# One decoder layer on one core: both heads' attention scores in one two-bank PSUM tile, small products issued as unbroken runs

## The chip, the cores and the metric

The kernel runs on one core of one Trainium2 chip. The metric is the device time of one execution in microseconds (us): lower is better. The time before is a median of three runs. A change of less than 0.2% (about 0.9 us) can't be told from none with this kernel.

## The reference, cut to what matters

The layer takes x (256 positions, 1024 channels, float32). After an RMS norm, one wide projection gives the queries, keys and values of three attention mixers with 64 channels a head, and merge gates; the mixers' outputs are projected, gated, merged, projected once more and added to x. Then come a gated feed-forward layer with a short convolution and a final norm.

```
def decoder(x):
    h = rmsnorm(x);  all = h @ w_in                      # q, k, v of A, B, C, and gates
    o_a = banded attention, 3 groups of 2 heads          # one softmax over all bands per head
    o_b = gate0 * compressed + gate1 * selected + gate2 * window    # 6 query heads, 2 kv heads
    o_c = causal attention, 4 heads
    x = x + (sum of sigmoid(gate) * (o @ w_branch)) @ w_out
    x = x + (silu(conv(u)) * conv(v)) @ w_down           # u, v = rmsnorm(x) @ w_up
    return rmsnorm(x)

# scores of one head: a query tile of 128 positions against the keys that it may see
s = q @ k.T * 0.125 + bias[distance];  p = softmax(s);  o = p @ v

# compression of B: 15 overlapping blocks of 32 positions, flattened to 2048, for k and for v
hidden = gelu(flat @ w1)      # (15 * 2 heads, 2048) @ (2048, 256)
cmp = hidden @ w2
```

## The kernel before, in words

**Projections.** Activations lie with channels on the partitions, split into a high and a low part (`hn_hi`, `hn_lo`). Weights come in units of up to 1 MB (`raw`), are split by ScalarE (`whi`, line 223) and VectorE (`wlo`, line 227), and each product of a projection is three matmuls into a PSUM tile `g` (`mm3`, lines 239 to 241), mostly 128 by 128 against 256 columns. There are four buffers of `raw`, two of each split, two PSUM banks of `g`. These projections fill TensorE for most of the kernel.

**Attention.** `scores` (line 437) computes one pair of heads. A pair lies in one 128-partition tile, head 0 on partitions 0 to 63 and head 1 on 64 to 127, and so its products contract over 64 rows. Two blocks are needed for causal attention: the first 128 queries against 128 keys (128 columns), the last 128 queries against 256 keys (256 columns). Each float32 product is two TensorE instructions, so that a pair of heads makes eight. The scores of each head go to a PSUM tile `s` of its own, of one bank; the pool `ps_s` has two. VectorE reads them with `add_max` (line 447: adds the bias, takes the maximum, writes to SBUF), ScalarE takes the exponentials (491 or 518), VectorE scales (498 or 522), TensorE transposes (454) into PSUM tile `t`, ScalarE copies to `pT` (456), and `pv` (462) multiplies with the values into PSUM tile `o`, which `put_o` (478, 479) evicts. The softmax of B and C works in SBUF tiles `tt`, of which there are three.

`scores` is called 11 times: three times for mixer A (loop at line 506), six for B (line 626: three pairs, selected and window branch each), two for C (line 643). One more user of `s` is B's compressed branch: two tiles, one for each half of the queries (line 596). The first projection also borrows one (line 382).

**Compression.** `hidden(i)` (line 532) loads one eighth of `w1` (512 KB, tile `gl`, four buffers, line 535) and multiplies it in four products that use 32 columns of the array each, into one PSUM tile `ph`. The first four eighths come ahead of unit b0, the other four between b0 and b1; the first of all has `start`, the last `stop`.

**Order.** The program is traced in this order, and a planner then fixes each engine's order ahead of time: it keeps a simulated clock, and an engine takes, of the instructions whose inputs are ready by that clock, the one with the lowest priority number, which is the order of tracing. Each engine then runs its list strictly in that order and waits at semaphores. In `manual_schedule` the instructions of a block keep the order in which they were traced on the engines named, but others may come between them. Projections of later units are therefore put between attention's products as filler. Memory and PSUM of the mixers are given back after the gates of the first half are traced (line 659), and the branch projections (line 722) come after that.

Of the kernel before, what the change touches and what calls it, by code (L numbers as in the profile page):

```python
# [10 lines left out]
F32 = mybir.dt.float32  # L11
# [5 lines left out]
P = 128  # L17
WARM = 16
S = 256
# [72 lines left out]
def _unit_places():  # L92

    at, places = 0, {}
    for name, _, rows, cols in _unit_list():
        k, n = sum(r for _, r in rows) // P, sum(c for _, c in cols)
        places[name] = (at, k, n)
        at += P * k * n
    return places, at
# [28 lines left out]
def decoder_layer(ctx: ExitStack, tc, x, small_b, table, w1, wts, norms, out):  # L128
    nc = tc.nc
    out = out[0]  # L130
    places, _ = _unit_places()
# [6 lines left out]
    psg = ctx.enter_context(tc.tile_pool(name="psg", bufs=2, space=bass.MemoryType.PSUM))  # L138
# [96 lines left out]
    def unit(name, steps=2, eng=None):  # L235
        return Unit(name).split(steps, eng)
# [6 lines left out]
    mix = ctx.enter_context(tc.tile_pool(name="mix", bufs=1))  # L243
    o_hi = mix.tile([P, KC, S], F32R, name="o_hi")
    o_lo = mix.tile([P, KC, S], F32R, name="o_lo")
    mixer = ctx.enter_context(ExitStack())
    qkv = mixer.enter_context(tc.tile_pool(name="qkv", bufs=1))
    att = mixer.enter_context(tc.tile_pool(name="att", bufs=1))
    ps_s = mixer.enter_context(tc.tile_pool(name="ps_s", bufs=2, space=bass.MemoryType.PSUM))
    ps_t = mixer.enter_context(tc.tile_pool(name="ps_t", bufs=2, space=bass.MemoryType.PSUM))  # L250
    ps_o = mixer.enter_context(tc.tile_pool(name="ps_o", bufs=2, space=bass.MemoryType.PSUM))


    idle = att.tile([P, 384], F32, name="tt", bufs=3)[:, :P]
# [83 lines left out]
    def chunk_T(view, pool=psg):  # L338

        ps = pool.tile([P, 512], F32, name="g")[:, :S]  # L340
        for i, k in enumerate(K_ORDER):
            mm3(ps, view(0, k), view(1, k), h_hi[:, k, :], h_lo[:, k, :], i == 0, i == KC - 1)
        return ps

    def chunks_hi_first(views, pss):

        half_k = range(KC // 2), range(KC // 2, KC)
        for a, b, ks in ((0, h_hi, range(KC)), (1, h_hi, half_k[0]), (0, h_lo, half_k[0]),
                         (1, h_hi, half_k[1]), (0, h_lo, half_k[1])):
            for k in ks:  # L350
                for view, ps in zip(views, pss):
                    nc.tensor.matmul(ps, view(a, k), b[:, k, :], start=(a == 0 and b is h_hi and k == 0),
                                     stop=(b is h_lo and k == KC - 1))

    def to_sbuf(ps, name, scale=1.0):
        o = qkv.tile([P, S], F32, name=name)
        nc.scalar.activation(o, ps, AF.Copy, scale=scale)
        return o

    def plain(u, c):  # L360
        return lambda part, k: u[part][:, k, c * P:(c + 1) * P]
# [17 lines left out]
    for i in range(3):  # L379
        if i == 0:  # L380
            u = u_a0.views
            pss = [p.tile([P, 512], F32, name=n)[:, :S] for p, n in ((psg, "g"), (ps_s, "s"))]
            chunks_hi_first([plain(u, c) for c in range(2)], pss)
        else:
            u = u_a1.views if i == 1 else unit(f"a{i}")
            pss = [chunk_T(plain(u, c)) for c in range(2)]
        for c in range(2):
            j = 2 * i + c
            aT.append(to_sbuf(pss[c], f"aT{j}", 0.125 if j < 3 else 1.0))
# [32 lines left out]
    flat = att.tile([P, 2, 16, 32], F32, name="flat")  # L422
    nc.vector.memset(flat, 0.0)
    for w in range(2):
        ps = chunk_T(plain(u, w))
        for kv in range(2):
            for odd in range(2):
                rows = slice(64 * odd, 64 * odd + 64)
# [5 lines left out]
    V1 = proj_V("v1", 512, "V1")  # L434


    def scores(q, k):

        pss = [ps_s.tile([P, 512], F32, name="s")[:, :384] for _ in range(2)]
        for q0, k1, o in ((0, P, slice(0, 128)), (P, S, slice(128, 384))):  # L440
            for i in range(2):
                rows = slice(64 * i, 64 * i + 64)
                nc.tensor.matmul(pss[i][:, o], q[rows, q0:q0 + P], k[rows, 0:k1], start=True, stop=True)  # L443
        return pss

    def add_max(dst, ps, bias, m):
# [12 lines left out]
    def o_tile():  # L459
        return ps_o.tile([P, 512], F32, name="o")[:, :S]  # L460

    def pv(po, terms, more=()):

        steps = []
        for pT, v, v0 in terms:
            steps.append([(slice(0, S), v[:, 0, v0[h]:v0[h] + 64], pT[h][:, 0:256]) for h in range(2)])
            steps.append([(slice(P, S), v[:, 1, v0[h]:v0[h] + 64], pT[h][:, 256:384]) for h in range(2)])
        steps += [[(slice(0, S), *m[h]) for h in range(2)] for m in more]  # L470
        with tc.manual_schedule(engines={mybir.EngineType.PE}):
            for i, step in enumerate(steps):
                for h in (1, 0):
                    cols, a, b = step[h]
                    nc.tensor.matmul(po[64 * h:64 * h + 64, cols], a, b, start=i == 0, stop=i == len(steps) - 1)  # L475

    def put_o(po, c):
        nc.scalar.activation(o_hi[:, c, :], po, AF.Copy)
# [46 lines left out]
    for g in range(3):  # L525
        po = o_tile()
# [2 lines left out]

    ph = o_tile()  # L530

    def hidden(i):

        wt = mix.tile([P, 4, S], F32, name="gl", bufs=4)
        nc.sync.dma_start(wt, w1[i])
        for grp in range(4):
            nc.tensor.matmul(ph[32 * grp:32 * grp + 32, :], flat[:, grp // 2, 2 * i + grp % 2, :], wt[:, grp, :],  # L537
                             start=(i == 0), stop=(i == 7))

    for i in range(4):  # L540
        hidden(i)


    u = unit("b0")
    bq = [to_sbuf(chunk_T(plain(u, c)), f"bq{c}", 0.125) for c in range(2)]
    for i in range(4, 8):
        hidden(i)
    u = unit("b1")
    bq.append(to_sbuf(chunk_T(plain(u, 0)), "bq2", 0.125))
    bks = to_sbuf(chunk_T(plain(u, 1)), "bks")  # L550
# [41 lines left out]


    pcT = att.tile([96, 2, S], F32, name="pcT")
    for t in range(NT):
        ps = ps_s.tile([P, 512], F32, name="s")[:, :96]
        for c in range(3):
            nc.tensor.matmul(ps[:, 32 * c:32 * c + 32], bq[c][:, t * P:(t + 1) * P], kcmp, start=True, stop=True)
        ps = ps.rearrange("p (c kv b) -> p kv c b", c=3, kv=2)
        wide = att.tile([P, 6, 32], F32, name="sc", bufs=2)  # L600
        nc.vector.memset(wide, 0.0)
        sc = wide[:, :, 0:16]
        mk = sb_[:, B_MK + 32 * t:B_MK + 16 + 32 * t][:, None, :].to_broadcast([P, 3, 16])
        ok = sb_[:, B_MK + 16 + 32 * t:B_MK + 32 + 32 * t][:, None, :].to_broadcast([P, 6, 16])
        for kv in range(2):
            nc.vector.tensor_add(sc[:, 3 * kv:3 * kv + 3, :], ps[:, kv], mk)
        m = small.tile([P, 6], F32, name="m6")
        nc.vector.tensor_reduce(m, sc[:, :, 0:15], axis=AX.X, op=ALU.max)
        nc.vector.tensor_sub(sc, sc, m[:, :, None].to_broadcast([P, 6, 16]))
        nc.scalar.activation(sc, sc, AF.Exp)  # L610
        z = small.tile([P, 6], F32, name="z6")
        nc.vector.tensor_reduce(z, sc[:, :, 0:15], axis=AX.X, op=ALU.add)
        nc.vector.tensor_mul(z, z, gsel[:, t, :, 0])
        nc.vector.reciprocal(z, z)
        nc.vector.tensor_mul(sc, sc, ok)
        nc.vector.tensor_mul(sc, sc, z[:, :, None].to_broadcast([P, 6, 16]))
        pp = ps_t.tile([P, 512], F32, name="t")[:96, :S].rearrange("p (a q) -> p a q", a=2)
        for a in range(2):
            nc.tensor.transpose(pp[:, a, :], wide[:, 3 * a:3 * a + 3, :].rearrange("p h b -> p (h b)"), ident)
        nc.vector.tensor_copy(pcT[:, :, t * P:(t + 1) * P], pp)  # L620

    for c in range(3):
        po = o_tile()
        pT = {}
        for w, k in ((1, bks), (2, bkw)):
            for kv, ps in enumerate(scores(bq[c], k)):
                h = c + 3 * kv
# [13 lines left out]
    for j in range(2):  # L641
        po = o_tile()
# [5 lines left out]
    def gates(i, pool):  # L648

        gl = [pool.tile([P, 4, S], F32, name="gl", bufs=4)[:, 0:3, :] for _ in range(2)]  # L650
        for b in range(3):
            u = unit(f"g{i}{b}")
            for c in range(2):
                nc.scalar.activation(gl[c][:, b, :], chunk_T(plain(u, c)), AF.Copy)  # L654
        return gl

    gl = {i: gates(i, mix) for i in range(2)}
# [7 lines left out]
    def gtile():  # L665
        turn[0] ^= 1
        return pools[turn[0]].tile([P, 512], F32, name="g")[:, :S]
# [34 lines left out]
    for i in range(4):  # L702
# [10 lines left out]
        for c in range(2):  # L713
# [5 lines left out]
            for b, (k0, k1) in enumerate(branch_k):  # L719
                ps = gtile()  # L720
# [25 lines left out]
    rows, scaled = spare[1][:, 0:S], [spare[1][:, i * S:(i + 1) * S] for i in range(1, 4)]  # L746
# [43 lines left out]
    with tc.manual_schedule(engines={mybir.EngineType.Activation, mybir.EngineType.DVE, mybir.EngineType.Pool,  # L790
# [49 lines left out]
        for i in range(4):  # L840
            for k in range(KC):
                u = fu[("fa0", "fu0")[i % 2]]
                nc.tensor.matmul(firsts[i], u[1][:, k, i // 2 * P:(i // 2 + 1) * P], h_hi[:, k, :], start=False,  # L843
                                 stop=k == KC - 1)
# [21 lines left out]
    for i in range(NFF // 2):  # L866
        with tc.issue_after(on_act[3 + i].ins) if i in (1, 2) else ExitStack():
            ua, uu, ud = [fu.pop(f"f{w}{i}", None) or unit(f"f{w}{i}") for w in "aud"]
        for c in range(2):
            ch = 2 * i + c  # L870

            def up(u):
                ps = gtile()
                for k in range(KC):
                    mm3(ps, u[0][:, k, c * P:(c + 1) * P], u[1][:, k, c * P:(c + 1) * P],
                        h_hi[:, k, :], h_lo[:, k, :], k == 0, k == KC - 1)
                return by_rstd(ps)
            a = conv(firsts[2 * ch] if ch < 2 else up(ua), ch)
            sa = mpool.tile([P, S], F32, name="sa")
            nc.scalar.activation(sa, a, AF.Silu)  # L880
            b = conv(firsts[1] if ch == 0 else by_rstd(firsts[3]) if ch == 1 else up(uu), NFF + ch)
# [45 lines left out]
```

## Time and profile before

| what | us |
|---|---|
| median of 3 runs | 437.43 (437.16 to 437.55) |
| profiled execution, its own time | 438.12 |
| span of its instructions | 436.3 |
| TensorE busy (matmuls) | 426.7 |
| VectorE busy | 306.9 |
| ScalarE busy | 240.8 |

The profiled execution is 0.69 us above the median of the runs, and its time is 1.8 us above its span. In the rows below, PE is TensorE, PEld its loading of weights, DVE VectorE, ACT ScalarE and SPq the queue that issues DMAs. `x8` counts instructions. Matmuls are pipelined: a row's duration runs until its last result, so one starts while those before it still run, and what a product takes from TensorE is read from one start to the next.

### The profile page before, as it was taken

How to read it: one execution, taken by the hardware profiler on the slowest of the kernel's cores; microseconds unless marked ns; L12 is line 12 of the kernel's file. 1: busy time of each engine (PE TensorE's matmuls, PEld its weight loads, DVE VectorE, ACT ScalarE, POOL GpSimd, SP SyncE). 2: the span in 40 equal slices, each digit the busy share in tenths (PEclk: the TensorE clock that was granted, in tenths of full speed). 3: DMA queues.
4: the chain of work that ended last, by engine and by line, in shares of the span. 5: the costliest groups of instructions: out<-in, count | busy, mean ns of one | idle time of the engine just before them, and what ended most of it. 6: DMA issues, size and time to landing. Idle time of an engine off the chain costs nothing.

```text
span 436.3 us, 7726 instructions
## 1 busy us (share of the span) xinstructions
PE 426.7 (98%) x3104; PEld 390.5 (89%) x3104; DVE 306.9 (70%) x637; ACT 240.8 (55%) x421; POOL 12.9 (3%) x19
## 2 busy tenths in 40 slices
PE   8999999999999999999999999999999999999993
PEld 7998877987789998999998998999999999999982
DVE  5756752888575588647535899897797797887854
ACT  6443362558676782456344769465465464573423
POOL 3301000000000000000000000000000000000001
PEclk9999999999999999999999999999999999999997
DMA  8988647340226785525550185753652743700002
GB/s 290 388 333 317 227 160 264 116 174 15 84 97 243 290 335 206 220 108 194 194 192 2 50 337 183 299 202 131 246 201 95 285 173 118 290 0 2 2 0 96
DMA packets 12611, 78.09 MB, mean 179 GB/s; under 512 B 1392, under 2 KB 1408, under 8 KB 4640
## 3 DMA queue, kind: packets, MB, share of 16 engines
q1 hardware_dynamic: 12000, 75.48, 46.6%
q0 software_dynamic: 576, 2.12, 1.4%
q8 instruction: 24, 0.39, 0.4%
q14 instruction: 11, 0.09, 0.1%
HBM read 76.52 MB, written 1.07 MB: 178 GB/s over the span
## 4 chain that ended last, share of the span: by engine, by line
PE 93%; DMA 2%; issue 1%; POOL 1%; DVE 1%; ACT 1%; POOLq 0%; SPq 0%
PE g L241 21%; PE g L239 21%; PE g L240 21%; PE acc L239 6%; PE acc L240 6%; PE acc L241 6%; PE s L443 3%; PE o L475 2%; PE t L454 2%; PE g L787 2%; DMA raw<-in_wts_dram 2%; PE o L537 1%; PE g L843 1%; POOL wlo L227 1%; PE acc L760 0%
## 5 line engine op out<-in xcount | busy, mean ns | idle before, releaser
L227 DVE TENSOR_TENSOR wlo<-raw,whi 128x1024 fp32r<-128x1024 f32 (+2 forms) x130 | 152.9, 1205 | 50.4 <-ACT whi L223 49.9
L239 PE MATMUL g<-hn_hi,wlo 128*128 128x256 f32 x632 | 180.6, 286 | 0.0
L241 PE MATMUL g<-hn_hi,whi 128*128 128x256 f32 x632 | 179.9, 285 | 0.0
L240 PE MATMUL g<-hn_lo,whi 128*128 128x256 f32 x632 | 179.9, 285 | 0.0
L223 ACT ACTIVATE whi<-raw 128x1024 fp32r<-128x1024 f32 (+2 forms) x130 | 129.3, 1038 | 38.2 <-PE g L241 28.1
L239 PEld LDWEIGHTS g<-hn_hi,wlo 128*128 128x128 f32 x632 | 121.1, 192 | 3.8 <-issue 2.3
L240 PEld LDWEIGHTS g<-hn_lo,whi 128*128 128x128 f32 x632 | 121.0, 192 | 2.7 <-issue 1.9
L241 PEld LDWEIGHTS g<-hn_hi,whi 128*128 128x128 f32 x632 | 121.1, 192 | 1.4 <-issue 1.3
L862 DVE SCALAR_TENSOR_TENSOR cy<-xn,small_b,cy 128x255 f32<-128x255 f32 (+1 forms) x88 | 41.7, 480 | 10.8 <-ACT cy L860 9.8
L860 ACT ACTIVATE cy<-xn,small_b 128x256 f32<-128x256 f32 x44 | 26.1, 594 | 17.2 <-DVE xn L776 17.2
L239 PE MATMUL acc<-whi,fl 128*128 128x512 f32 x88 | 34.5, 393 | 0.0
L240 PE MATMUL acc<-wlo,fh 128*128 128x512 f32 x88 | 34.4, 391 | 0.0
L241 PE MATMUL acc<-whi,fh 128*128 128x512 f32 x88 | 34.2, 389 | 0.0
L885 ACT ACTIVATE fh<-sa 128x256 fp32r<-128x256 f32 x22 | 9.1, 413 | 33.1 <-DVE sa L882 33.1
L776 DVE TENSOR_TENSOR xn<-g,xn 128x256 f32<-128x256 f32 x44 | 18.5, 420 | 9.6 <-PE g L241 9.0
L654 ACT ACTIVATE gl<-g 128x256 f32<-128x256 f32 x24 | 9.1, 381 | 24.1 <-PE g L241 24.1
L241 PEld LDWEIGHTS acc<-whi,fh 128*128 128x128 f32 x88 | 16.5, 188 | 3.6
L239 PEld LDWEIGHTS acc<-whi,fl 128*128 128x128 f32 x88 | 16.6, 188 | 3.1
L240 PEld LDWEIGHTS acc<-wlo,fh 128*128 128x128 f32 x88 | 16.6, 189 | 2.8
L240 PE MATMUL g<-o_lo,whi 128*128 128x256 f32 x64 | 18.1, 283 | 0.0
L241 PE MATMUL g<-o_hi,whi 128*128 128x256 f32 x64 | 18.1, 283 | 0.0
L239 PE MATMUL g<-o_hi,wlo 128*128 128x256 f32 x64 | 18.1, 283 | 0.0
(180 smaller groups left out, 505.4 us busy)
## 6 DMA issues: line engine op xcount, KB each, us to landing
raw<-in_wts_dram SPq DMA_DIRECT2D x62, 1024.0 KB, 4.9
gl<-in_w_dram SPq DMA_DIRECT2D x8, 512.0 KB, 7.5
raw<-in_wts_dram SPq DMA_DIRECT2D x2, 804.0 KB, 8.3
raw<-in_wts_dram SPq DMA_DIRECT2D x3, 512.0 KB, 7.2
T<-tvd POOLq DMA_DIRECT2D x1, 1280.0 KB, 13.3
xs<-in_x_dram SPq DMA_DIRECT2D x2, 516.0 KB, 3.8
out_dram<-raw SPq DMA_DIRECT2D x4, 256.0 KB, 2.2
T<-tvd POOLq DMA_DIRECT2D x1, 768.0 KB, 8.2
```

The source lines that it names most:

```text
L223: nc.scalar.activation(self.parts[0][:, sl], self.raw[:, sl], AF.Copy)
L227: return (eng or nc.vector).tensor_sub(self.parts[1][:, sl], self.raw[:, sl], self.parts[0][:, sl].bitcast(F32))
L239: nc.tensor.matmul(ps, al, bh, start=start, stop=False)
L240: nc.tensor.matmul(ps, ah, bl, start=False, stop=False)
L241: nc.tensor.matmul(ps, ah, bh, start=False, stop=stop)
L443: nc.tensor.matmul(pss[i][:, o], q[rows, q0:q0 + P], k[rows, 0:k1], start=True, stop=True)
L454: nc.tensor.transpose(ps[:, i * P:(i + 1) * P], b, ident)
L654: nc.scalar.activation(gl[c][:, b, :], chunk_T(plain(u, c)), AF.Copy)
L776: nc.vector.tensor_mul(u, ps, rows)
L860: on_act.append(nc.scalar.activation(y, u, AF.Identity, bias=vec_c[:, 3, ch:ch + 1], scale=vec_c[:, 2, ch:ch + 1]))
L862: nc.vector.scalar_tensor_tensor(y[:, sh:], u[:, :S - sh], vec_c[:, w, ch:ch + 1], y[:, sh:], op0=ALU.mult, op1=ALU.add)
L885: nc.scalar.activation(fh, sa, AF.Copy)
```

## The change

Both heads of a pair now share one tile `s` of two banks (one bank for each head), of which there is one. The compressed branch's two tiles are the two banks of one such tile, and the first projection takes one bank of one. A helper `together` issues a list of products in a manual block in which all but the first have the highest priority. `scores`, `pv` and `hidden` use it. `hidden` is called twice, for four eighths at a time: it loads all four, then multiplies, the last loaded first, so that `start` and `stop` move to eighths 3 and 6. The products, their operands and their number are the same.

```diff
-    ps_s = mixer.enter_context(tc.tile_pool(name="ps_s", bufs=2, space=bass.MemoryType.PSUM))
+    ps_s = mixer.enter_context(tc.tile_pool(name="ps_s", bufs=1, space=bass.MemoryType.PSUM))
+    def s_tile():
+        return ps_s.tile([P, 2, 512], F32, name="s")
...
-            pss = [p.tile([P, 512], F32, name=n)[:, :S] for p, n in ((psg, "g"), (ps_s, "s"))]
+            pss = [psg.tile([P, 512], F32, name="g")[:, :S], s_tile()[:, 0, :S]]
...
+    def together(products):
+        with tc.manual_schedule(engines={mybir.EngineType.PE}):
+            products[0]()
+            with tc.high_priority():
+                for p in products[1:]:
+                    p()
+
     def scores(q, k):
-        pss = [ps_s.tile([P, 512], F32, name="s")[:, :384] for _ in range(2)]
-        for q0, k1, o in ((0, P, slice(0, 128)), (P, S, slice(128, 384))):
-            for i in range(2):
-                rows = slice(64 * i, 64 * i + 64)
-                nc.tensor.matmul(pss[i][:, o], q[rows, q0:q0 + P], k[rows, 0:k1], start=True, stop=True)
+        both = s_tile()
+        pss = [both[:, i, :384] for i in range(2)]
+        def product(i, q0, k1, o):
+            rows = slice(64 * i, 64 * i + 64)
+            nc.tensor.matmul(pss[i][:, o], q[rows, q0:q0 + P], k[rows, 0:k1], start=True, stop=True)
+        together([lambda x=(i, *blk): product(*x) for blk in ((0, P, slice(0, 128)), (P, S, slice(128, 384)))
+                  for i in range(2)])
...
-        with tc.manual_schedule(engines={mybir.EngineType.PE}):
-            for i, step in enumerate(steps):
-                for h in (1, 0):
-                    cols, a, b = step[h]
-                    nc.tensor.matmul(po[64 * h:64 * h + 64, cols], a, b, start=i == 0, stop=i == len(steps) - 1)
+        def product(i, h):
+            cols, a, b = steps[i][h]
+            nc.tensor.matmul(po[64 * h:64 * h + 64, cols], a, b, start=i == 0, stop=i == len(steps) - 1)
+        together([lambda x=(i, h): product(*x) for i in range(len(steps)) for h in (1, 0)])
...
-    def hidden(i):
-        wt = mix.tile([P, 4, S], F32, name="gl", bufs=4)
-        nc.sync.dma_start(wt, w1[i])
-        for grp in range(4):
-            nc.tensor.matmul(ph[32 * grp:32 * grp + 32, :], flat[:, grp // 2, 2 * i + grp % 2, :], wt[:, grp, :],
-                             start=(i == 0), stop=(i == 7))
-    for i in range(4):
-        hidden(i)
+    def hidden(eighths):
+        wt = {}
+        for i in eighths:
+            wt[i] = mix.tile([P, 4, S], F32, name="gl", bufs=4)
+            nc.sync.dma_start(wt[i], w1[i])
+        def product(i, grp):
+            nc.tensor.matmul(ph[32 * grp:32 * grp + 32, :], flat[:, grp // 2, 2 * i + grp % 2, :], wt[i][:, grp, :],
+                             start=(i == 3), stop=(i == 6))
+        together([lambda x=(i, grp): product(*x) for i in (eighths[3], *eighths[:3]) for grp in range(4)])
+    hidden(range(4))
     u = unit("b0")
...
-    for i in range(4, 8):
-        hidden(i)
+    hidden(range(4, 8))
...
+    both = s_tile()
     for t in range(NT):
-        ps = ps_s.tile([P, 512], F32, name="s")[:, :96]
+        ps = both[:, t, :96]
```

## Rows read from the trace of the kernel before

**Rows 1.** The page, part 1: each engine's busy time.

```profile
PE 426.7 (98%) x3104; PEld 390.5 (89%) x3104; DVE 306.9 (70%) x637; ACT 240.8 (55%) x421; POOL 12.9 (3%) x19
```

**Rows 2.** Busy time by stretch: start:end, length, then each engine.

```profile
84.00:112.00 28.00, 28.00 (x197) 21.32 (x197) 24.00 (x122) 19.54 (x61) 0.00 (x0) 1.00 0.31 113
112.00:131.00 19.00, 18.85 (x159) 15.62 (x156) 11.16 (x51) 12.89 (x40) 0.00 (x0) 1.00 0.15 56
131.00:260.00 129.00, 129.00 (x991) 124.64 (x988) 83.07 (x122) 73.46 (x110) 1.08 (x2) 1.00 0.53 198
260.00:423.00 163.00, 163.00 (x1145) 153.21 (x1145) 132.70 (x220) 93.02 (x139) 0.00 (x0) 1.00 0.41 151
```

**Rows 3.** PE in order of time (start, duration): a call with both heads at once.

```profile
86.19 0.28 PE L241 MATMUL g<-hn_hi,whi 128*128 128x256 f32 x1
86.40 0.93 PE L443 MATMUL s<-bks,bq 64*128 64x128 f32 x8
87.27 0.39 PE L239 MATMUL g<-hn_hi,wlo 128*128 128x256 f32 x1
87.49 0.28 PE L240 MATMUL g<-hn_lo,whi 128*128 128x256 f32 x1
87.61 0.28 PE L241 MATMUL g<-hn_hi,whi 128*128 128x256 f32 x1
```

**Rows 4.** PE in order of time: one head of a call alone.

```profile
91.47 0.28 PE L240 MATMUL g<-hn_lo,whi 128*128 128x256 f32 x1
91.68 0.92 PE L443 MATMUL s<-bkw,bq 64*128 64x128 f32 x4
92.53 0.39 PE L241 MATMUL g<-hn_hi,whi 128*128 128x256 f32 x1
92.75 0.28 PE L239 MATMUL g<-hn_hi,wlo 128*128 128x256 f32 x1
```

**Rows 5.** Busy time of line 443 alone, by stretch: PE, PEld, clock, DMA.

```profile
47.00:49.50 2.50, 1.48 (x8) 1.03 (x8) 1.00 0.55 210
49.50:52.00 2.50, 1.05 (x8) 0.65 (x8) 1.00 0.03 7
89.00:111.50 22.50, 9.49 (x40) 5.10 (x40) 1.00 0.27 99
120.70:123.00 2.30, 1.45 (x8) 1.03 (x8) 1.00 0.00 0
```

**Rows 6.** PE in order of time: the first of five half-head pieces.

```profile
100.23 0.48 PE L443 MATMUL s<-bkw,bq 64*128 64x128 f32 x2
100.64 1.52 PE L475 MATMUL o<-pT,V 128*64 128x256 f32 x16
```

**Rows 7.** Busy time of line 537 alone, by stretch: first and second four eighths.

```profile
62.00:65.00 3.00, 1.93 (x32) 0.94 (x32) 1.00 0.94 359
67.50:75.00 7.50, 2.56 (x32) 0.63 (x32) 1.00 0.63 232
```

**Rows 8.** SPq and PE in order of time: the second four eighths' DMA issues and first products.

```profile
63.31 1.75 SPq L535 DMA_DIRECT2D gl<-in_w_dram  x4
...
68.02 0.64 PE L537 MATMUL o<-gl,flat 128*32 128x256 f32 x8
```

**Rows 9.** The page, part 6: DMA issues, KB each, median us to landing.

```profile
gl<-in_w_dram SPq DMA_DIRECT2D x8, 512.0 KB, 7.5
```

**Rows 10.** DVE and PE in order of time, with idle time before and its releaser.

```profile
95.51 0.29 DVE L447 CUSTOM_DVE_ANT_0 tt<-s,T 128x128 f32<-128x128 f32 x1 [0.55 <-PE t L454]
...
121.13 1.45 PE L443 MATMUL s<-cT,cT 64*128 64x128 f32 x8 [0.15 <-DVE m L447]
...
121.52 1.22 DVE L227 TENSOR_TENSOR wlo<-raw,whi 128x1024 fp32r<-128x1024 f32 x1
```

**Rows 11.** Tiles `o_lo` and `o_hi`: ns min/median/max, first and last start.

```profile
L479 DVE TENSOR_TENSOR o_lo<-o,o_hi x8: 416/423/426, 60.7 to 132.9; 128x256 fp32r<-128x256 f32 x8
L239 PE MATMUL g<-o_hi,wlo x64: 277/283/283, 160.0 to 231.2; 128*128 128x256 f32 x64
```

## Prediction

> **What bounds the kernel now.** I read the page first: TensorE is busy for 98% of the span, VectorE for 70%, ScalarE for 55% [rows 1]. Since durations of matmuls overlap, 98% does not say that time can't be taken out of TensorE, only that no engine starves it. The table by stretch says where each limit lies [rows 2]. From 84 us on TensorE is busy in every stretch but for 0.15 us of the one from 112 to 131. VectorE comes near it in one place: 24.00 of 28 us between 84 and 112, where B's attention runs; from 112 to 131 it is busy for 11.16 of 19 us, in the two long stretches after that for 83.07 of 129 and 132.70 of 163 us. So the time is TensorE's instruction stream laid end to end, and what counts is how long a piece of that stream keeps the next one from starting. That is read in TensorE's order of time, from start to start.
>
> **What a call of scores costs today.** Around 86 us the eight instructions of a pair of heads come in one run [rows 3]. Filler products start 0.12 us apart (87.49 to 87.61). From the last filler product at 86.19 to the second one after the scores at 87.49 are 1.30 us; two pitches of 0.12 are filler's own, so the call costs 1.06 us: its busy time of 0.93 and about 0.13 for going in and coming out (the first score starts 0.21 after its predecessor in place of 0.12, and the first filler product after them takes 0.22).
> Around 91.7 us the four instructions of one head stand alone [rows 4]: from 91.47 to 92.75 are 1.28 us, less 0.24: 1.04 us. One head costs what both cost. In [rows 3] the two heads, which use different halves of the array's rows, run side by side; alone, a head leaves half the array idle. This is the point of the whole case.
>
> **The change, part by part.**
>
> *Scores of B.* The first of the six calls is whole already [rows 3]. The other five (40 instructions between 89 and 111.5 us) keep TensorE busy for 9.49 us [rows 5], in twelve pieces: seven single heads like the one in [rows 4] and five half heads, of which the first stands in [rows 6]. They are apart because each head's bank came free at its own time. With one tile for both heads the products of a call become ready together, and with the highest priority on all but the first nothing comes between. Five whole calls are busy for 5 x 0.93 = 4.65 us: 4.84 less. Pieces fall from twelve to five. Two of the seven at the full 0.12 for going in and out give 0.24; the five half heads mostly stand beside transposes or the values' products, which are plain float32 as well and must be changed to anyway (from 100.23 to 100.64 the half head takes 0.41 up to the values' products), so I give them 0.05 each, 0.25. Sum: **5.3 us**. Bounds: 4.8 (no change of mode counts) and 5.7 (all seven at 0.12).
>
> *Scores of A and C.* A's second and third call are in one run each, but head after head or staggered: busy 1.48 and 1.05 in place of 0.93, and C's second call 1.45 [rows 5]. Issued in pairs they give 0.55 + 0.12 + 0.52 = **1.2 us**. A's and C's first calls are whole. Bounds: 0.6, if half of the stagger stays because TensorE takes up the pairs unevenly, and 1.3 with the 0.15 us of waiting in front of C's second call [rows 10].
>
> *Compression.* The first four eighths are one run, busy 1.93 us; the second four are four runs, busy 2.56 us together [rows 7]. One run saves 0.63, and three times going in and out at 0.12 saves 0.36: **1.0 us**. DMAs: the same eight loads of 512 KB on the same queue, in the same order; only the products wait for the last of four in place of each for its own. The other end of this term is the rival below.
>
> *At nothing.* The values' products are in one run already (sixteen instructions from 100.64 [rows 6], and so at all eight places), so the new priority has nothing to gather. The compressed branch's scores keep their two banks. Moving `start` and `stop` moves no work. One bank of a two-bank tile for the first projection is the same bank.
>
> *The new wait.* A call now waits until both heads of the call before have been read, where one head's bank was enough. Behind the waiting instruction stands all of TensorE's list, filler included. If the planned place is late enough, the wait costs nothing, since filler stands ahead of it; the rows show how well the plan hits it: 0.15 us of waiting in front of C's second call, with an `add_max` as the releaser [rows 10]. Eight calls get such a wait (two of A, five of B, one of C; B's first waits for the compressed branch as before). The lower end is 0, the upper end one split of VectorE in front of the last `add_max`, 1.22 us [rows 10], at each. The row nearest to it is the 0.15; I take half of it as the mean, 8 x 0.075 = 0.6, less the 0.15 that goes: **0.4 us** lost.
>
> *Evacuation.* VectorE's reading of the scores is not shortened at all. In B an `add_max` waits, 0.55 us at 95.5, for transposes of an earlier head [rows 10], which release one of the three `tt` buffers: attention there has a pace of its own, which this change doesn't touch. What takes up the 5.3 us is filler, pulled ahead. There is enough: the last `o_lo` of attention is written at 132.9, and the first branch product, which needs it, starts at 160.0 [rows 11], so 27 us of gate products lie between, four times the gain; loads, splits and VectorE (11.16 of 19 us) have room for one more unit in 112 to 131.
> The Trainium skill speaks against this (TensorEngine Tiling, Performance Considerations, PSUM Bottleneck): using the array in tiles speeds up TensorE but not the reading of PSUM, which may become the bottleneck. By it the 5.3 and C's 0.52 would be lost, and 0.67 + 1.0 would stay: 436.4 us on the scale of the profiled execution. By the rows, TensorE is busy for all of 84 to 112 though attention waits at `tt`, so the sum stands with 5.3.
>
> **Sum.** 5.3 + 1.2 + 1.0 - 0.4 = 7.1 us. The profiled execution took 438.12 us, so it would take 431.0. It stands 0.69 above the median of 437.43; on the median's scale, to which I predict, that is 430.3, rounded to 430.4.
>
> **Rivals.**
>
> *Attention's pace wins (gain 1.7 to 5).* The evacuation above, in full or in part: TensorE has the time but no filler that is split and ready. For it: 86% of VectorE from 84 to 112, and each unit of filler wants two splits of 1.22 us. Against it: no idle TensorE in that stretch today, and 27 us of outstanding filler. In full, B's 5.3 and C's 0.52 are lost, and A's 0.67 and compression's 1.0 stay: 437.4 - 1.7 = 435.7. With half of B's gain kept it is 433.
>
> *The four eighths come too early.* The group needs the last of four loads. They are issued from 63.31 to 65.06, and the median landing is 7.5 us after issue, so the last one is in at about 72.2 [rows 8, 9]. The first eighth's products ran at 68.02 [rows 8]. If the plan puts the group there, TensorE stands for 4.2 us and the gain is 7.1 - 4.2 = 2.9: 434.5. Against it: the planner places a product where it takes its data to have landed, and the four runs of today came in step with their loads.
>
> *Slower: the wait at the head of the list.* If the plan has VectorE read a call's scores sooner than it does, TensorE stands with filler behind it. Only splits of 1.22 us are long enough to push an `add_max` that far back, and one of them follows directly on the last `add_max` at 121.52 [rows 10]. From 7.5/8 = 0.94 us per call on, the gain is gone; at 1.22 it costs 9.8 us, and the time is 437.4 - 7.5 + 9.8 = 439.7. For it: eight places, and a VectorE that is nearly full. Against it: 0.15 us at the place that has this form today. The Trainium skill gives the rule that makes it possible (TensorE: Matmul & The Clock Gate, The mechanism, under Packing small matmuls): matmuls start and end strictly in their order, none passes another.
>
> *It doesn't do what it says.* The scores stay in pieces, since the plan finds a pair not ready in one go. Then only compression's 1.0 is left, and waits eat it: within 0.2% of 437.4. Against it: both heads read the same tiles of queries and keys and write one tile, so they are ready at one time.
>
> **How the numbers follow.** The forecast, a gain of 6.0 (lower bounds of B, A and C, with the waits as taken) to 8.0 (upper bounds, no waits), has 0.60: 429.4 to 431.4. A gain beyond that, from filler that packs better, 0.06. Attention's pace 0.13, the early group 0.08, the change without effect 0.05, slower 0.08. Faster by over 0.2% (0.9 us) is 0.60 + 0.06 + 0.13 + 0.08 = 0.87, the same 0.05, slower 0.08. For 8 in 10 I go from 428.8 to 434.7: the forecast whole, half of those beyond it, the early group and the milder half of attention's pace.
>
> **What the changed kernel's profile would show.** Line 443's products as eleven runs of eight, each busy for 0.93 us, 10.2 us in all; compression's second four eighths as one run of 32, busy 1.93, starting after 72 us; no releaser `m` of VectorE with more than 0.3 us in front of a run of scores; TensorE still without idle time from 84 to 131; the last `o_lo` at about 133 as today, later by a few us at most; and the first product of `o_hi` some 7 us earlier, at 153. The stretches after that keep their lengths. I am wrong if scores stay in pieces, if idle time of TensorE with VectorE or a DMA as its releaser adds up to more than 2 us before 131, or if the 7 us are there at `o_hi`'s first product and are lost again later, because a load or a split can't follow.

## The result: 5.1 us faster

The changed kernel takes 432.24 us (median of 4 runs, 431.95 to 432.60) against 437.33 us for the one before: the ratio is 0.9881, with a 95% interval of 0.9869 to 0.9893. Measured once more beside the last experiment it took 432.11 us against 437.56, a ratio of 0.9874 (0.9859 to 0.9888). The forecast was 430.4: the measured time lies outside the narrower range that the prediction gave it (429.4 to 431.4, at 0.60) and inside the wider one (428.8 to 434.7, for 8 in 10). The profiled execution took 432.46 us, 5.66 less than the one before, and its span went from 436.3 to 430.7 us.

The page, part 1, of the changed kernel answers to [rows 1]: TensorE is busy for 5.9 us less, and the other engines have the work that they had.

```profile
PE 420.8 (98%) x3104; PEld 388.3 (90%) x3104; DVE 307.1 (71%) x637; ACT 240.0 (56%) x421; POOL 12.9 (3%) x19
```

In the new line numbers, 455 issues the scores (443 before), 462 is `add_max`, 469 the transposes, 471 the copy to `pT`, 488 the values' products, 506 ScalarE's exponentials, 510 to 513 VectorE's scaling, 555 compression's products. TensorE in order of time, around A's second and third call:

```profile
49.39 0.93 PE L455 MATMUL s<-aT,aT 64*128 64x128 f32 x8
50.24 0.39 PE L241 MATMUL g<-hn_hi,whi 128*128 128x256 f32 x1
...
51.78 0.28 PE L241 MATMUL g<-hn_hi,whi 128*128 128x256 f32 x1
51.99 0.93 PE L455 MATMUL s<-aT,aT 64*128 64x128 f32 x8
52.85 0.38 PE L239 MATMUL g<-hn_hi,wlo 128*128 128x256 f32 x1
```

Both are the form of [rows 3], where the same two calls were busy for 1.48 and 1.05 us [rows 5]. Of all scores, busy time by stretch (PE, PEld, clock, DMA), the kernel before first:

```profile
44.00:140.00 96.00, 16.25 (x88) 9.39 (x88) 1.00 0.43 155
```

```profile
44.00:140.00 96.00, 10.19 (x88) 5.76 (x88) 1.00 0.44 164
```

The same 88 instructions keep TensorE busy for 10.19 us, 6.06 less; every one of the 11 calls is one run of eight. Compression's second four eighths are one run too, where [rows 7] had four of 2.56 us in all:

```profile
74.09 0.34 PE L241 MATMUL g<-whi,hn_hi 128*128 128x402 f32 x1
74.36 1.93 PE L555 MATMUL o<-gl,flat 128*32 128x256 f32 x32
76.23 0.45 PE L239 MATMUL g<-whi,hn_lo 128*128 128x402 f32 x1
```

The end of attention and the start of the branch products, which answers to [rows 11]:

```profile
L239 PE MATMUL g<-o_hi,wlo x64: 277/283/386, 154.3 to 225.5; 128*128 128x256 f32 x64
L494 DVE TENSOR_TENSOR o_lo<-o,o_hi x8: 417/422/425, 62.4 to 128.9; 128x256 fp32r<-128x256 f32 x8
```

The first product of `o_hi` starts at 154.34 in place of 160.02, 5.7 us earlier; from there to the end of the span are 276.4 us, 276.3 before. So the whole gain is made before 154 us and none is lost later. Attention itself ends 4.0 us earlier, not later.

Busy time of all engines by stretch (PE, PEld, DVE, ACT, POOL), with the stretches of [rows 2], the last two moved by the 5.7 us:

```profile
84.00:112.00 28.00, 27.13 (x225) 22.68 (x224) 24.48 (x122) 18.51 (x60) 0.00 (x0) 1.00 0.39 148
112.00:131.00 19.00, 18.75 (x161) 14.82 (x161) 13.11 (x60) 13.27 (x41) 0.00 (x0) 1.00 0.12 28
...
125.30:254.30 129.00, 129.00 (x991) 124.48 (x990) 83.08 (x123) 74.22 (x112) 1.08 (x2) 1.00 0.53 198
254.30:417.30 163.00, 163.00 (x1146) 153.19 (x1145) 132.73 (x220) 93.06 (x139) 0.00 (x0) 1.00 0.41 151
```

The last two are as before. The first two show what is new: TensorE, which had 0.15 us of idle time there, now has 0.87 + 0.25 = 1.12.

**Where it stands.** TensorE waits in front of transposes. The longest place, TensorE in order of time, with idle time and its releaser:

```profile
98.89 0.28 PE L239 MATMUL g<-hn_hi,wlo 128*128 128x256 f32 x1
99.59 0.30 PE L469 MATMUL t<-ident,tt 128*128 128x128 f32 x1 [0.42 <-ACT tt L506]
99.65 0.37 PE L240 MATMUL g<-hn_lo,whi 128*128 128x256 f32 x1
```

VectorE ahead of it, then ScalarE:

```profile
98.76 0.16 DVE L510 TENSOR_TENSOR z<-z,ge 128x2 f32<-128x2 f32 x1 [0.92 <-ACT tt L506]
...
99.16 0.55 DVE L513 TENSOR_SCALAR tt<-tt,r 128x128 f32<-128x128 f32 x2
```

```profile
96.99 0.49 ACT L471 ACTIVATE pT<-t 128x384 f32<-128x384 f32 x1 [1.36 <-PE t L469]
97.38 0.39 ACT L506 ACTIVATE tt<-tt,nm 128x128 f32<-128x128 f32 x1
...
97.77 0.48 ACT L471 ACTIVATE pT<-t 128x384 f32<-128x384 f32 x1
98.14 0.50 ACT L506 ACTIVATE tt<-tt,nm 128x256 f32<-128x256 f32 x1
```

The transpose at 99.59 needs the scaled `tt` of 99.16, whose first block is done at 99.45. (This profile names ScalarE's exponential as the releaser, which ends at 99.51; in the profile of experiment 10 the same place, at 99.30 there, has VectorE's scaling, line 513.) VectorE had waited 0.92 us for ScalarE's exponentials, and among these ScalarE makes two copies to `pT`, 0.49 and 0.48 us. The filler product at 99.65 belongs to the same group of three as the one at 98.89, so its unit was there; it stood behind the transpose in the list. From 44 to 131 us TensorE is idle for 1.31 us, at eight places. Those of more than 0.15 us are these (us in total, times, longest); an `ACT pT` as the releaser is the copy that frees a bank `t`:

```profile
PE t L469 <- ACT tt L506: 0.4, 1, 0.4
PE t L469 <- ACT pT L471: 0.3, 1, 0.3
```

The other six are 0.04 to 0.15 us long: three in front of transposes, and one each in front of a call of scores (0.07, A's second, behind an `add_max`), of values' products (0.13, for a `pT`) and of filler (0.12).

**The sum of TensorE's stream.** Each product counted from its own start to the next one's, from 20 us to the first branch product:

| products | before | after | difference |
|---|---|---|---|
| scores | 15.00 | 9.62 | -5.38 |
| compression's eighths | 4.14 | 3.73 | -0.41 |
| filler with 402 columns beside the eighths | 9.79 | 9.13 | -0.66 |
| filler with 256 columns | 80.84 | 81.54 | +0.70 |
| transposes of `tt` and `t` | 6.27 | 6.37 | +0.10 |
| all, with those not listed | 139.94 | 134.27 | -5.67 |

A wait is counted with the product ahead of it, and so is the change of form, which is the time that TensorE loses in going from filler to a small product: the first one starts 0.21 us after the filler ahead of it [rows 3], where filler follows filler after 0.12. Hence filler grows although its work is the same.

### The profile page after: what moved, and what is told of

Read it like the earlier page. It is cut to its first block, busy times and chain, and to the rows that moved or that the text cites. A ratio compares the mean times of both kernels' runs of the same rounds, so it can differ in the third digit from the quotient of the medians.

```text
span 430.7 us, 7724 instructions
## 1 busy us (share of the span) xinstructions
PE 420.8 (98%) x3104; PEld 388.3 (90%) x3104; DVE 307.1 (71%) x637; ACT 240.0 (56%) x421; POOL 12.9 (3%) x19
## 3 DMA queue, kind: packets, MB, share of 16 engines
HBM read 76.52 MB, written 1.07 MB: 180 GB/s over the span
## 4 chain that ended last, share of the span: by engine, by line
PE 90%; ACT 3%; issue 2%; DMA 2%; DVE 1%; POOL 1%; POOLq 0%; SPq 0%; ACTq 0%
PE g L239 21%; PE g L241 20%; PE g L240 20%; PE acc L239 6%; PE acc L240 6%; PE acc L241 6%; PE o L488 2%; PE t L469 2%; PE g L806 2%; DMA raw<-in_wts_dram 2%; PE s L455 1%; PE g L862 1%; PE o L555 1%; ACT tt L506 1%; POOL wlo L227 1%
```

## Experiments

Each kernel was compared with runs of the kernel before on its own chip (437.50 to 437.57 us). The edits are shown against the whole change, or, in experiment 3, against the kernel before, cut to the lines that matter.

**1. The two-bank tile alone.** `scores` issues its products without a block and without priority; `pv` and `hidden` are as before.

```diff
-        together([lambda x=(i, *blk): product(*x) for blk in ((0, P, slice(0, 128)), (P, S, slice(128, 384)))
-                  for i in range(2)])
+        for q0, k1, o in ((0, P, slice(0, 128)), (P, S, slice(128, 384))):
+            for i in range(2):
+                nc.tensor.matmul(pss[i][:, o], q[rows, q0:q0 + P], k[rows, 0:k1], start=True, stop=True)
```

> Only the shared two-bank tile; products of a call are in no manual block, values' products and eighths are as before. Theory (the tile makes both heads ready at one time, and that alone lines them up): the scores are busy for about 10.2 us as with the whole change, and the time is the whole change's 432.2 plus the 1.0 us of compression: 433.2, within 0.8. Rival (the priority keeps the run together, without it filler comes between): scores in more than 20 pieces, busy for 13 us or more, time 435.5 to 437.4.

Measured: 436.14 us, ratio 0.9963 (0.9950 to 0.9976). The scores come in 16 pieces: eight of the eleven calls are whole, but transposes and values' products still get between the products of the other three. Busy time of the scores:

```profile
44.00:140.00 96.00, 12.79 (x88) 6.99 (x88) 1.00 0.43 156
```

12.79 us is just over half way from 16.25 to 10.19. Part of what that gives is lost elsewhere: transposes take 0.8 us more from start to start, and the new plan puts one eighth too early for its load:

```profile
69.23 0.34 PE L241 MATMUL g<-whi,hn_hi 128*128 128x402 f32 x1
70.51 0.64 PE L541 MATMUL o<-gl,flat 128*32 128x256 f32 x8 [0.93 <-DMA gl<-in_w_dram]
```

Neither theory holds whole: the tile gathers more than the rival said, and the time is the rival's.

**2. Priority without the tile.** One-bank tiles, two of them, with `scores` in `together`; the rest as before.

```diff
-        both = s_tile()
-        pss = [both[:, i, :384] for i in range(2)]
+        pss = [ps_s.tile([P, 512], F32, name="s")[:, :384] for _ in range(2)]
```

> The counterpart of the tile alone: a call's products in one manual block with the priority, but each head in a bank of its own as before; values' products and eighths as before. Theory (what lines the heads up is that both banks come free at one time; the priority only keeps together what is ready): the first product of head 0 goes alone when its bank is free, the other three products in a second piece when head 1's is, so most calls are in two pieces. Each such call costs about 0.5 us more than a whole one; B's five then cost 7.4 in place of 10.6 us, and the time is some 2.6 us under before: 434.2 to 436. Rival (the priority is enough): calls whole, 432.2 + 1.0 = 433.2, within 0.6.

Measured: 437.19 us, ratio 0.9998 (0.9983 to 1.0013): no gain that can be told from none. Nine of the eleven calls come in two pieces, the first product when one bank is free, the other three when the second is:

```profile
90.21 0.48 PE L450 MATMUL s<-bkw,bq 64*128 64x128 f32 x2
...
92.11 0.92 PE L450 MATMUL s<-bkw,bq 64*128 64x128 f32 x6
```

Six instructions, of which four belong to head 1 and two to head 0, take what all eight take in [rows 3], so the early product saves nothing. The tile is needed, as the theory said; its size (2.6 us of gain) was wrong. B's five calls do take 2.3 us less from start to start, each 0.42 + 0.85. But A's third and B's first call, of 0.98 and 0.86 us before, are cut in two as well, for 0.7 us more, and with 20 pieces in place of 18 the other products' lines grow by 1.7. From the first score to the first branch product that leaves 0.3 us. So tile and priority need each other: alone they give 1.4 us and nothing that stands out of the noise.

**3. Compression's eighths alone.** `hidden` in two groups with `together`, all else as before.

```diff
-    for i in range(4):
-        hidden(i)
+    hidden(range(4))
...
-    for i in range(4, 8):
-        hidden(i)
+    hidden(range(4, 8))
```

> Only compression's eighths in two groups (with their order and the priority); scores as before. Theory (0.63 us of busy time and three times going in and out of their mode): 1.0 us less than before, 436.3, within 0.5, and 32 products in one run after 72 us. Rival (the group waits for the last of four loads with all of TensorE behind it): TensorE idle in front of the group for over 0.5 us, and 436.8 to 440.

Measured: 436.65 us, ratio 0.9984 (0.9975 to 0.9993), 0.9 us less, as forecast for this term.

**4. Head after head in the list.** The whole change, but a call lists both products of head 0, then both of head 1.

```diff
-        together([lambda x=(i, *blk): product(*x) for blk in ((0, P, slice(0, 128)), (P, S, slice(128, 384)))
-                  for i in range(2)])
+        together([lambda x=(i, *blk): product(*x) for i in range(2)
+                  for blk in ((0, P, slice(0, 128)), (P, S, slice(128, 384)))])
```

> The whole change, but within a call's run the products go head after head (both of head 0, then both of head 1): the same eight instructions in one run, the same number of changes of mode. Theory (the gain is that the heads run side by side on two halves of the array's rows): a run takes 1.40 in place of 0.86 us from start to start, as A's second call did before, 11 x 0.54 = 5.9 us, and the time is about 438.1, no gain left. Rival (the gain is fewer pieces and changes of mode, the order in a run is worth nothing): 432.2, within 0.5.

Measured: 432.20 us, ratio 0.9871 (0.9856 to 0.9885): the same as the whole change, and the theory fell. The scores' instructions of one call that were under way up to 0.30 us after its start at 88.72 (count, ns, first and last start, forms):

```profile
L455 PE MATMUL s<-bks,bq x4: 272/322/373, 88.7 to 89.0; 64*128 64x128 f32 x4
```

All four that have started have 128 columns, two for each head, though head 0's product of 256 columns stands ahead of head 1's first in the list. They start 0, 13, 213 and 226 ns after the first: head 1 does not wait for its turn behind head 0. The whole run is 862 ns long from its first start to the next filler product's, against 856 in the changed kernel. [Rows 3] could have hinted at this: there the second head starts 14 ns after the first and the run is 863 ns long, as here, where the changed kernel's has 7 and 856. So that call seems to have been listed head after head in the kernel before, and it took 0.93.

**5. Both heads on one half of the rows.** The whole change, but head 1 reads head 0's partitions: its scores are left out, and head 0's are computed twice.

```diff
-            rows = slice(64 * i, 64 * i + 64)
+            rows = slice(0, 64)
```

> The whole change, but the products of head 1 read the partitions of head 0, so that both use the same 64 rows of the array. It leaves out head 1's scores and computes head 0's twice. The same eight instructions in one run, the same pieces, the same banks. Theory (heads on different halves run side by side, whatever their order in the list, and this is where the gain is): a run takes 1.6 to 1.7 in place of 0.86 us from start to start, eleven times 0.8 = 8.8 us more, about 441. Rival (the gain is in fewer pieces and changes of mode): 432.2, within 0.8.

Measured: 437.27 us, ratio 0.9992 (0.9983 to 1.0001). A call in TensorE's order of time:

```profile
90.27 1.57 PE L455 MATMUL s<-bks,bq 64*128 64x128 f32 x8
91.77 0.42 PE L638 MATMUL t<-ident,sc 128*96 128x128 f32 x2
```

From its first start to the next product's are 1.50 us in place of 0.86: 0.65 more, 7.1 us in eleven calls. The time rose by 5.0, since the new waits went away at the same time. Busy time from 44 to 131 us (PE first), for this kernel and then for the whole change and for the kernel before:

```profile
44.00:131.00 87.00, 86.86 (x677) 73.81 (x675) 58.79 (x237) 49.31 (x134) 0.00 (x0) 1.00 0.37 134
```

```profile
44.00:131.00 87.00, 85.69 (x713) 71.58 (x712) 60.65 (x240) 50.58 (x136) 0.00 (x0) 1.00 0.40 145
```

```profile
44.00:131.00 87.00, 86.76 (x665) 69.39 (x665) 57.47 (x237) 48.94 (x133) 0.00 (x0) 1.00 0.39 141
```

TensorE is idle for 0.14, 1.31 and 0.24 us. That the time is that of the kernel before does not mean that joining pieces is worth nothing. B's five calls, which were in pieces, take 5 x 1.50 = 7.5 us here, 8.7 in the kernel before and 5 x 0.86 = 4.3 in the changed one: of the 4.4 us that the scores' own line gains there, 1.1 come from joining and 3.2, three quarters, from two heads on both halves of the array at a time. This kernel loses the 1.1 again, and more, at the calls that had run side by side before, such as A's, B's and C's first (3 x 0.65). And most of the waits are there only while TensorE is ahead.

**6. The transposes in one run.** The whole change, and each head's three transposes in `together`, the last block first.

```diff
-        for i, b in enumerate(blocks):
-            nc.tensor.transpose(ps[:, i * P:(i + 1) * P], b, ident)
+        def turned_block(i):
+            nc.tensor.transpose(ps[:, i * P:(i + 1) * P], blocks[i], ident)
+        together([lambda i=i: turned_block(i) for i in (2, 1, 0)])
```

> The whole change, and the three transposes of a head also issued as one run, the last block first (it is ready last). Theory (what is missing of the forecast are waits of TensorE in front of transposes whose input ScalarE and VectorE have late, and split transposes cost about 0.17 us for each further piece): pieces of transposes fall from about 22 to under 16, some 1 to 2 us less than the whole change: 430.2 to 431.4. Rival (the missing part is an unlike plan, not these waits and pieces): within 0.5 of 432.2, or slower, if the run now waits longer than the pieces did.

Measured: 432.92 us, ratio 0.9894 (0.9878 to 0.9910): no better than the whole change. From start to start the transposes take 7.34 us in place of 6.37, since the first now waits for what only the last one needed before: TensorE is idle for 1.72 us from 44 to 131, 1.5 of it in front of transposes that wait for VectorE's scaling.

**7. A fourth `tt` buffer.** The whole change with four `tt` in place of three; two small tiles share other buffers to make room.

```diff
-        return att.tile([P, 384], F32, name="tt", bufs=3)
+        return att.tile([P, 384], F32, name="tt", bufs=4)
```

> The whole change with four tt buffers in place of three (two small tiles of compression share the buffers of another to make room). Theory (TensorE's new waits in front of transposes come from ScalarE and VectorE being later than planned, whatever the buffers): within 0.6 us of the whole change's 432.2, waits still there. Rival (attention's pace is set by the three buffers, and the waits with it): waits under half, 431 or less.

Measured: 431.75 us, ratio 0.9868 (0.9855 to 0.9881), 0.5 under the whole change, with intervals that overlap. TensorE still waits, for 1.25 us between 89 and 128 (1.12 in the whole change). So the number of buffers is not what holds the transposes up.

**8. The copies to `pT` on VectorE.** The whole change, with the 22 copies taken from ScalarE.

```diff
-        nc.scalar.activation(o, ps, AF.Copy)
+        nc.vector.tensor_copy(o, ps)
```

> The whole change with the copy of the transposes out of PSUM (22 of them, 0.49 us each on ScalarE) moved to VectorE. Theory (the new waits in front of transposes go back to ScalarE's exponentials, which these copies hold up): waits of TensorE between 95 and 123 us fall from about 1.9 to under 1 us, time 430.8 to 431.7. Rival (VectorE is as late as ScalarE, the wait only moves): 432.2 or more.

Measured: 431.18 us, ratio 0.9856 (0.9842 to 0.9870), 1.1 us under the whole change as first measured (on one chip with it, and with four `tt`, 1.0: experiments 9 and 10). Busy time from 44 to 131 us, and the last `o_lo`:

```profile
44.00:131.00 87.00, 86.30 (x724) 73.48 (x725) 67.57 (x253) 42.97 (x109) 0.00 (x0) 1.00 0.45 159
```

```profile
L494 DVE TENSOR_TENSOR o_lo<-o,o_hi x8: 414/422/425, 64.2 to 140.6; 128x256 fp32r<-128x256 f32 x8
```

TensorE's idle time falls from 1.31 to 0.70 us. But the plan has changed too: attention ends at 140.6 in place of 128.9, so more filler lies between its products. Which of the two it is, ScalarE's shorter work or the wider spread, isn't told apart by this run. Experiment 9 narrows it: there, with four `tt` as well, attention ends at 134.6, and idle time (0.70) and time are the same, so the spread beyond 134.6 seems to be worth nothing.

**9 and 10. Both remedies together, beside the whole change on one chip.**

> Theory (the waits that the whole change brings stand at transposes and values' products, behind ScalarE, and each of the two remedies takes another part of them): copies of pT on VectorE gave 431.18, four tt buffers 431.75, the whole change 432.24; both together give 1.1 + 0.5 under the whole change, 430.3 to 431.0, close to the predicted 430.4. Rival (both remedies reach the same waits, so the second adds nothing): 431.0 to 431.6. If VectorE, which takes the copies, becomes the limit once more buffers let exponentials run ahead: above 431.6.

> The whole change unaltered, on the chip of the run beside it, so that the two versions stand against each other on one chip. Expected 431.9 to 432.6, as before.

Measured: 431.15 us, ratio 0.9854 (0.9838 to 0.9871), and 432.11 for the whole change. Copies on VectorE with four `tt` are 1.0 us better than the whole change on the same chip, and no better than the copies alone, as the rival said. That both reach the same waits is not shown by it: what four `tt` give alone, 0.5 us, is within the noise and may be nothing.

## Why the prediction was right, and where it was too large

**Direction and mechanism: right; the size: too large.** The eleven runs of eight, each busy for 0.93 us, 10.2 us in all, are there. Experiment 5 shows the reason that the prediction gave: with both heads on one half of the rows a call takes 1.50 us in place of 0.86, and three quarters of what B's five calls gain are gone. Experiments 1 and 2 show that the two-bank tile and the priority must come together for it. The priority of the values' products, which the prediction put at nothing, was not run by itself; from start to start they take 7.9 us, 8.1 before. The gain, 5.1 us, falls short of the 6.0 at which the forecast's own range ended; that it lies in the wider range it owes to the room left there for "attention's pace", and it did not come as that rival had it, for want of ready filler: at the longest wait the filler was there. Of the signs, the branch products come 5.7 us earlier in place of 7, and TensorE does have idle time from 84 to 131; the limit of 2 us for that is not reached.

**Scores: 6.1 in place of 6.5 (5.3 + 1.2).** Their busy time fell by 6.06 us; the prediction's terms without changes of form are 4.84 + 1.19 = 6.03. From start to start scores gave 5.38, and fewer changes of form lie in the filler's line. What these gave is only worked out, as what is left: 5.67 of the whole, less 1.07 for compression, plus 1.5 for the waits below, are 6.1. The starts agree: filler is followed by scores 8 times in place of 14, at 0.09 us each 0.5, and of the new waits 0.2 are counted with a score, so 5.4 + 0.5 + 0.2 = 6.1. So 0.4 too much was set for them, most of it the credit of 0.49 for going in and out. The prediction laid that price on plain float32, and this the trace does not bear out: the compressed branch's scores, float32 on the full array, start at 85.09 in the changed kernel, 0.12 us after the filler ahead of them, as filler would.

**Compression: 1.07 (0.41 + 0.66) for 1.0**, and alone 0.9. The run starts at 74.36, after its loads; the rival of the early group did not come to pass here. Experiment 1 shows that such a wait can arise: 0.93 us for one eighth.

**The new wait: the step that was mis-sized.** The prediction gave 0.4 us net, in front of the scores. By idle time TensorE lost 1.07 us more than before (1.31 less 0.24). By the gaps between starts, in which a product ahead hides part of a wait, my estimate is about 0.8 before and 2.3 after (each start against the usual distance of such a pair), 1.5 net; I take this one, as it goes with the table. It is also not where I put it: TensorE's longest idle time in front of scores with an `add_max` as its releaser is 0.07 us, while 0.99 of the 1.31 us stand in front of transposes, 0.42 of them at once. The prediction asked only what the scores wait for. When their 6 us leave the stream, everything that ScalarE and VectorE owe to the next products is due sooner, and the work behind a run of scores (exponentials, sums, scaling) was not sped up; this reading is the one that experiment 5 supports. That is the part of "attention has a pace of its own" that the prediction named and then costed at nothing, because filler was to take up the time. The filler was there, as the product at 99.65 shows, but behind the waiting transpose. Experiment 5 shows that these waits come with TensorE's being ahead, 7 that they don't come from the three `tt`, 8 that taking copies from ScalarE and spreading attention over more filler takes 0.6 us off TensorE's idle time and 1.1 off the kernel's.

So of the 1.4 us between 7.1 and 5.67, by the estimate of 1.5, about 1.1 are waits and 0.4 are scores, with 0.1 the other way from compression. On medians the gain is 5.1 and 5.5 us; for the first of these, the profiled execution of before stands 0.8 above the median of the result and that of after 0.2.

**Attention's pace.** Forecast was that the last `o_lo` would stay at about 133 us. It came at 128.9: a good part of attention's pace had been TensorE's own. The reading of PSUM did not become the limit either: VectorE is busy for 24.48 of 28 us, where it was busy for 24.00 [rows 2], and the scores' gain is kept. Of TensorE's 1.31 us of idle time 0.38 (0.25 + 0.13) wait for copies out of PSUM to `pT`. Here the trace does not bear out that the rule of the Trainium skill (TensorEngine Tiling, Performance Considerations, PSUM Bottleneck) decides; by it 436.4 us were worked out.

**The slower rival** rested on TensorE's list being held up at its head. In kind that happened, for 0.4 us at the longest single idle time and at transposes, far from 0.94 at each of eight calls.

**A's and C's second calls** were long for another reason than the lower bound of their term had it. The prediction feared that the order of the pairs might keep half of the stagger. Experiment 4 shows that the order doesn't matter. What did is in the trace of before, VectorE in order of time:

```profile
47.54 0.42 DVE L447 CUSTOM_DVE_ANT_0 t<-s,T 128x256 f32<-128x256 f32 x1
```

It reads the first call's last bank until 47.96, while the second call has begun at 47.47; head 1 starts at 48.03, 0.56 us after head 0, which is the 0.55 by which that call is longer than 0.93. C's second call has the same form: `add_max` reads until 121.60, head 1 starts at 121.66, 0.53 us after head 0, and 0.52 is its excess. With one tile for both, head 0 no longer starts alone.

## What to carry to other kernels

Two small products that use different halves of the array cost what one costs, if they are issued together; so look in TensorE's order of time for pieces in which one half works alone, and take the price of each from its own rows (here a head alone 0.85 us, half a head 0.42 to 0.63, both heads together 0.86). To keep them together, make them ready together (one tile, one release) and let nothing be planned between them: here neither alone did it in full. When TensorE's stream gets shorter, price what the other engines owe to the products that are next in its list, also where the edit touches nothing: filler that stands behind them in a fixed order does not help.

## What was not expected of the hardware

In experiment 4 products on different halves of the rows start in another order than that in which the kernel lists them: head 1's 128 columns start 13 ns after head 0's and about 0.3 us before head 0's 256 columns, which stand ahead of them. The Trainium skill (TensorE: Matmul & The Clock Gate, Packing small matmuls, The mechanism) has matmuls start strictly in their order; the trace differs from it here, and the measurement decides.

A call with three of its four products left (0.85 us from its first start to the next product's, experiment 2, at 92.11) takes as long as one with all four (0.86).
